# In-projection of a hybrid DiT backbone: own buffers for the mLSTM decays, and outputs that follow the states without a stop

## The chip, the cores and the metric

The kernel runs on one core of one Trainium2 chip. The metric is the device time of one execution in microseconds (us). A core has five engines that run at the same time and in their own order, and that wait for one another through semaphores: TensorE (PE, with its weight loads as PEld), VectorE (DVE), ScalarE (ACT), GpSimd (POOL) and SyncE (SP), which here issues the DMAs.

## The reference

Two layers over 1024 latent and 256 context tokens of width 1024. Each layer normalises and modulates the tokens, projects them once (`h @ w_in`) and splits the columns into attention (aq, ak, av), a bidirectional mLSTM in chunks of 128 tokens (mq, mk, mv, mo, gates) and a pooling mixer (pp); the three outputs are concatenated, projected back, and a SwiGLU follows. The part around the change is the mLSTM's chunk loop:

```
def step(carry, inp):                       # one chunk, one direction
    C, n, m = carry
    ...
    s = einsum('bhtd,bhsd->bhts', qc, kc) * exp(dmat - m_t[..., None])
    num = w_inter[..., None] * einsum('bhvk,bhtk->bhtv', C, qc) + einsum('bhts,bhsv->bhtv', s, vc)
    den = w_inter * einsum('bhk,bhtk->bht', n, qc) + sum(s, -1)
    h = num / maximum(abs(den), exp(-m_t))[..., None]
    ...
    C_new = a[..., None, None] * C + einsum('bhs,bhsv,bhsk->bhvk', wk, vc, kc)
    n_new = a[..., None] * n + einsum('bhs,bhsk->bhk', wk, kc)
def mlstm_readout(h, o_pre, ml_norm):
    hn = rms_norm(h, ml_norm)
    return hn * sigmoid(o_pre)
```

## The kernel before, in words

All matmuls are three products of f16 halves. The in-projection is a row of gemms, one after the other, which feed PE: `gemm_fm` (features by tokens, matmuls `pfm` at L492, in passes of 12 or 24) and `gemm_tm` (tokens by features, matmuls `ptm` at L497). Their order is O_MK, O_MQ, gates, O_MV, O_MO, O_MQ+P, then pooling's first half (`pool_gemm(0)`), O_AK, O_AQ 0, `pool_gemm(1)`, O_AQ 1 to 3 and last O_AV. Beside them run threads, Python generators that `spawn` puts in a list and that are stepped between pieces of a gemm; `drain(t)` steps a thread to its end at once. The kernel's own statement order and a scheduler behind it then fix the order on each engine.

The threads of the mLSTM are these. `ml_states` (`stg`) makes 18 state steps in each layer, 9 chunks by 2 directions. A step's `front` transposes k on PE (`pk`, 4 matmuls, L931), weighs it on DVE (`kw`) and splits it into f16 halves on ACT and POOL (`kh`); its `back` multiplies on PE (`pu`, 12 matmuls, L945), updates the state `C` on DVE and stores it as `snap`. `ml_outputs(z)`, z = 0 and 1, makes the outputs of the even and of the odd chunks, so the two threads go in pairs of chunks: five pairs in layer 0 (context too) and four in layer 1. One chunk (`ml_chunk`) loads its gates `sgc` and row `mrow`, multiplies q by k (`pst`), and for each direction makes the mask and bias on PE (`pm`, L998 and L999) and the exponentials `E` on ACT (L1000 and the `act` under it), weighs `pst` by E on DVE, and splits E into f16 halves `Ah` on ACT and POOL. `inter` multiplies by the state (`pxi`, L1024), `intra` multiplies `Ah` by v (`pi`, L1038), adds on DVE into `num`, makes the divisor `dn`, and the quotient `T<-num,dn`. Behind the second direction come the sum of both, the square on ACT, its sum (`s<-T`), the root on ACT and six small operations, the two gains, the split into `oh` (ACT, then DVE), and two stores `mld<-oh` (L1083), four for a pair of chunks.

Work tiles come from one pool `w` for the phase "g" (in-projection), and are freed at the start of phase "s" (attention), whose tiles lie over them. Among them is a ring `f2k` of 8 buffers of 2 KB for a partition, which holds E, `kw`, the `q` and `sqq` of the attention's keys and queries (`c_qk`), and others; a new tile waits until the readers of the tile 8 before are done. PSUM has 8 banks in this phase.

In phase "s" the mLSTM's and pooling's outputs are read back (`DMA_TRANSPOSE T<-mld` at L1317, `T<-pld`, `X<-xs`), and the attention goes by units: scores on PE (`Sp`, L1337), their maximum on DVE (`mx<-Sp`), the exponentials on ACT (`pf`), f16 halves (`phl`), a transpose by DMA (`pT<-phl`, L1366), the product with v (`pv`, L1379). The out-projection (`pwo`, L1400) fills PE between units. It needs `T<-mld` and `T<-pld`. DMAs on SP's queue are issued in the order that is written. In the views a tile's name stands without its number, and one name can cover several tiles: `T<-mld` is the part of `mixT`, and `T`, `X` are also other work tiles.

Of the kernel before, what the change touches and what calls it, by code (L numbers as in the profile page):

```python
# [9 lines left out]
F32 = mybir.dt.float32  # L10
# [8 lines left out]
P = 128  # L19
# [62 lines left out]
def hybrid_kernel(ctx: ExitStack, tc: tile.TileContext, I, out, dbg=None):  # L82
    nc = tc.nc
    order = mybir.DependencyInfo(mybir.DependencyClass.NoSync, mybir.DependencyReason.DATA)
    row = {"on": False, "last": None}

    class InRow:

        def __init__(self, e):
            self.e = e  # L90

        def __getattr__(self, name):
            f = getattr(self.e, name)

            def call(*a, **k):
                b = f(*a, **k)  # L96
                if row["on"]:
                    if row["last"] is not None:
                        tc.add_manual_dep(b.ins, row["last"].name, order, reason="written order")
                    row["last"] = b.ins  # L100
                return b
            return call

    def in_row(on):
        row.update(on=on, last=None)

    V = InRow(nc.vector)
    S, G, TE, DMA = nc.scalar, nc.gpsimd, nc.tensor, nc.sync
    MUL, ADD, SUB, MAX, MIN = ALU.mult, ALU.add, ALU.subtract, ALU.max, ALU.min
    dbg = dbg or {}  # L110

# [4 lines left out]


    cur = {}
    F2K = {"g": 8, "s": 6}
    PFB, PHB, PTB = 2, 3, 5  # L120

    def phase(kind):
# [19 lines left out]
    def bank(name="bk"):  # L142
        return cur["b"].tile([P, 512], F32, tag="bk", name=name)
# [8 lines left out]
    def pt_(shape, dt, tag, bufs=1, name=None):  # L152
        return cur["w"].tile(list(shape), dt, tag=tag, name=name or tag, bufs=bufs)

    def f2k(shape=(P, 512), dt=F32, name="f2k"):
        return pt_(shape, dt, "f2k", F2K[cur["kind"]], name)

# [33 lines left out]
    def stt(o, a, s, b, o0, o1):  # L191
        V.scalar_tensor_tensor(o, a, s, b, op0=o0, op1=o1)

    def tt(o, a, b, op, e=None):
        (e or V).tensor_tensor(o, a, b, op=op)  # L195

# [5 lines left out]
    threads = []  # L202

    def spawn(gen):
        threads.append(gen)
        return gen
# [12 lines left out]
    def pump(n=1):  # L219
        for _ in range(n):  # L220
            for g in list(threads):
                try:
                    next(g)
                except StopIteration:
                    threads.remove(g)

    def drain(g=None):
        while (g in threads) if g is not None else threads:
            if g is None:
                pump()  # L230
            else:
                try:
                    next(g)
                except StopIteration:
                    threads.remove(g)
# [16 lines left out]
    def x_tile(i):  # L252
# [3 lines left out]
        for g in range(2):  # L256
# [6 lines left out]
            else:  # L263
                V.tensor_copy(o, i_)

# [18 lines left out]
    cs_f = con.tile([P, 16], F32, name="cs_f")  # L284
    V.tensor_scalar(cs_f, cvec, -85.0, None, op0=MAX)
    act(cs_f, cs_f, AF.Exp, scale=-1.0)
    V.tensor_scalar(cs_f, cs_f, 1.0, None, op0=ADD)
    V.reciprocal(cs_f, cs_f)
    tt(cs_f, cs_f, cvec, MUL)
# [248 lines left out]
    def rstd(ms, n, u, r0=None):  # L538

        if r0 is None:  # L540
            r0 = f2k((P, 512), F32, "r0")
        act(r0[:, :n], ms, AF.Ln, bias=epsc)
        act(r0[:, :n], r0[:, :n], AF.Exp, scale=-0.5)
        act(u[:, :n], r0[:, :n], AF.Square)
        stt(u[:, :n], ms, EPS, u[:, :n], ADD, MUL)
        V.tensor_scalar(u[:, :n], u[:, :n], -0.5, 1.5, op0=MUL, op1=ADD)
        tt(r0[:, :n], r0[:, :n], u[:, :n], MUL)
        return r0
# [218 lines left out]
    for l in range(DEPTH):  # L767
        last = l == DEPTH - 1
# [203 lines left out]
        def ml_outputs(z):  # L972
            for c in range(z, nto, 2):
                yield from ml_chunk(c, z)

        def ml_chunk(c, z):
# [19 lines left out]
            def decay_(d):  # L996
                pm = bank("pm")
                mm(pm.rearrange("p (h t) -> p h t", h=4), idb, mskb[:, d].unsqueeze(1).to_broadcast([P, 4, P]), start=True, stop=False)  # L998
                mm(pm, one3, mrow[d], start=False, stop=True)  # L999
                E = f2k((P, 4, P), F32, "E")  # L1000
                for i, h in enumerate(HO):
                    r = d * 64 + c * 4 + h
                    act(E[:, i], pm[:, i * P:(i + 1) * P], AF.Exp, bias=tmq[:, 0, r:r + 1])
                Ev = E.rearrange("p h t -> p (h t)")
                for g in range(2):
                    stt(Ev[:, g * 256:(g + 1) * 256], pst[g][:, 0:256], 1.0 / 16, Ev[:, g * 256:(g + 1) * 256], MUL, MUL)
                Ah = pt_((P, 2, 4, P), F16, "Ah", 4)
                act(Ah[:, 0].rearrange("p h t -> p (h t)"), Ev)
                tt(Ah[:, 1], E, Ah[:, 0], SUB, G)
                Ahs.append(Ah)  # L1010
# [137 lines left out]
        def q_roots():  # L1148

            v = rq[:, :, :nto].rearrange("p a c h -> p a (c h)")  # L1150
            rstd(v[:, 0], nto * 8, v[:, 2], v[:, 1])
            V.tensor_scalar(v[:, 0], v[:, 1], 0.125 / 16, None, op0=MUL)
            V.tensor_scalar(v[:, 1], v[:, 1], -0.125 / 16, None, op0=MUL)
# [28 lines left out]
        def pool_tile(i, u):  # L1182
            S2, S4, S8, S16 = (1, 0), (1, 1), (2, 2), (4, 4)
            for (t0, n) in blks:
                ub = u[:, pcol(t0) - 8:pcol(t0) + n + 8]
                bA = pt_((P, 768), F32, "pb", 2, "bA")
                bB = pt_((P, 768), F32, "pb", 2, "bB")

                def win(o, s, sh, lo_, hi_, x):

                    tt(o[lo_:hi_, x:n + 16 - x], s[lo_:hi_, x - sh[0]:n + 16 - x - sh[0]],
                       s[lo_:hi_, x + sh[1]:n + 16 - x + sh[1]], ADD, G)

                if i == 0:
                    win(bA, ub, S2, 64, 128, 7)
                    win(bB, ub, S2, 0, 64, 8)
                    win(bB, bA, S4, 64, 128, 8)
                    fin = [bB, bB]
                else:
                    win(bA, ub, S2, 0, 128, 1)  # L1200
                    win(bB, bA, S4, 0, 128, 2)
                    yield
                    win(bA, bB, S8, 0, 128, 4)
                    win(bB, bA, S16, 64, 128, 8)
                    fin = [bA, bB]
                p = f2k((P, 512), F32, "pm")
                for g in range(2):
                    ps = slice(64 * g, 64 * g + 64)
                    f = fin[g][ps, 8:8 + n]
                    if t0 != 512:  # L1210
                        tt(f[:, 0:8], f[:, 0:8], edge[ps, i, 0:8], MUL, G)
                    if t0 != 0:
                        tt(f[:, n - 8:n], f[:, n - 8:n], edge[ps, i, 8:16], MUL, G)
                yield
                for g in ([0] if fin[0] is fin[1] else range(2)):
                    ps = slice(0, P) if fin[0] is fin[1] else slice(64 * g, 64 * g + 64)
                    stt(p[ps, :n], fin[g][ps, 8:8 + n], invw[ps, i:i + 1], ub[ps, 8:8 + n], MUL, SUB)
                yield
                pb = bank("ppool")
                mm(pb[:, :n], pw[:, i], p[:, :n], start=True, stop=True)  # L1220
                sc = ps16[:, l * 2 + i:l * 2 + i + 1]
                ph = f2k((P, 2, 512), F16, "ph")
                act(ph[:, 0, :n], pb[:, :n], scale=sc)
                stt(ph[:, 1, :n], pb[:, :n], sc, ph[:, 0, :n], MUL, SUB)
                DMA.dma_start(out=pld[:, i, :, t0:t0 + n], in_=ph[:, :, :n])
                yield
# [6 lines left out]
        for (t0, n) in BLOCKS:  # L1233
            if t0 in nx:
                drain(nx.pop(t0))
            for r in range(3):
                if t0 >= T and last and r == 2:
                    continue
                if l == 0 and t0 < T:
                    pb = pf0[r][t0 // 512]  # L1240
                else:
                    pb = bank("pfm")
                    fm(pb[:, :n], wf[r], h1, t0, n)
                held.append((r, t0, n, pb))
                pb = None
# [3 lines left out]
            while held and t0 > 0:  # L1249
                r_, t_, n_, pb = held.pop(0)  # L1250
                fst[r_](t_, n_, pb[:, :n_])
                pb = None
                pump()
        w = w_get(("in", l, O_MG))
        pb = bank("pmg")
# [11 lines left out]
        stg = ml_states()  # L1267
# [17 lines left out]
        for i in range(2):  # L1285
            DMA.dma_start(out=cst[i], in_=I["t_cs"][:, i])
        gemm_fm(O_MQ + P, blks, c_ml(qml, 1, INV * 4))
        drain(stg)
        spawn(ml_outputs(0))
        spawn(ml_outputs(1))  # L1290
        def pool_gemm(i):
            u = pool_u()

# [15 lines left out]
        while next_is_ada() or pend:  # L1309
            ada_fill()  # L1310
        drain()
        q_roots()


# [151 lines left out]
        for i in range(nu + 5):  # L1466
# [5 lines left out]
            if turns:  # L1472
                qt, g = turns.pop()
# [290 lines left out]
        sg, Sg, Su = sgs[0], f0.pop("Sg"), f0.pop("Su")  # L1764
        f0.clear()
        act(sg[:, :NTq], Sg[:, :NTq], AF.Silu, scale=INV)
        in_row(True)
        stt(sg[:, :NTq], Su[:, :NTq], 1.0 / SW, sg[:, :NTq], MUL, MUL)

        ho = h_ops()  # L1770
# [20 lines left out]
        for _ in ho:  # L1791
            pass
        drain()
        in_row(False)
        for k in range(4):
            split2(h2[:, k, :, H1], scv[:, k], V)

# [204 lines left out]
        for bi, (t0, n) in enumerate([(0, 512), (512, 256), (768, 256)] if last else blks):  # L2002
            sums = None if last else Sums(t0, n)
            for m in range(NK):
                w = piece("last", m)
                pb = bank("pdn")
# [8 lines left out]
            if bi == 0:  # L2015
# [3 lines left out]
                pb = None  # L2019
# [48 lines left out]
```

## Time and profile before

| | |
|---|---|
| median of 3 runs | 2776.61 us (2774.57 to 2776.82) |
| the profiled execution | 2780.47 us |
| its span | 2778.7 us |
| PE busy | 2564.7 us, 92% of the span |
| DVE busy | 1890.2 us, 68% |
| ACT busy | 1387.1 us, 50% |
| POOL busy | 1269.3 us, 46% |
| TensorE clock granted, mean | 0.969 |

The span is what the profiler sees of the program, and the rest of the execution, 1.8 us, lies around it. The profiled execution is 3.9 us above the median of the three runs. PE is the busiest engine; the clock that it was granted is given as a share of full speed.

### The profile page before, as it was taken

How to read it: one execution, taken by the hardware profiler on the slowest of the kernel's cores; microseconds unless marked ns; L12 is line 12 of the kernel's file. 1: busy time of each engine (PE TensorE's matmuls, PEld its weight loads, DVE VectorE, ACT ScalarE, POOL GpSimd, SP SyncE). 2: the span in 40 equal slices, each digit the busy share in tenths (PEclk: the TensorE clock that was granted, in tenths of full speed). 3: DMA queues.
4: the chain of work that ended last, by engine and by line, in shares of the span. 5: the costliest groups of instructions: out<-in, count | busy, mean ns of one | idle time of the engine just before them, and what ended most of it. 6: DMA issues, size and time to landing. Idle time of an engine off the chain costs nothing. (4 is left out here: it accounts for less than half of the span.)

```text
span 2778.7 us, 53623 instructions
## 1 busy us (share of the span) xinstructions
PE 2564.7 (92%) x21403; PEld 1500.9 (54%) x21403; DVE 1890.2 (68%) x3233; ACT 1387.1 (50%) x2650; POOL 1269.3 (46%) x963
## 2 busy tenths in 40 slices
PE   7999989987899999999999998888878899999997
PEld 4875556655555555555554684455545344444444
DVE  5558867778766555656565557866777767667676
ACT  5345557766443434444344544466765444444453
POOL 1124446774334435444443213456763465555651
PEclk9999999999899999999999999999989899999999
DMA  9544489995132222223212222389993111111211
GB/s 301 144 123 113 126 203 184 190 177 121 57 92 81 87 84 84 86 82 92 61 46 78 69 55 57 115 185 182 191 174 102 46 53 54 62 61 54 61 53 76
DMA packets 631629, 296.21 MB, mean 107 GB/s; under 512 B 362888, under 2 KB 620756, under 8 KB 630868
## 3 DMA queue, kind: packets, MB, share of 16 engines
q1 hardware_dynamic: 631204, 292.73, 42.9%
q8 instruction: 167, 2.74, 0.4%
q14 instruction: 82, 0.67, 0.1%
q10 hardware_dynamic: 176, 0.07, 0.0%
HBM read 176.19 MB, written 20.87 MB: 71 GB/s over the span
## 5 line engine op out<-in xcount | busy, mean ns | idle before, releaser
L1960 PEld LDWEIGHTS <-hlp 128*128 128x128 f16 x5040 | 492.0, 98 | 602.7 <-issue 26.6
L1960 PE MATMUL Swb<-T,hlp 128*128 128x512 f16 x1920 | 445.6, 381 | 18.5 <-DVE sg L96 13.0
L195 POOL TENSOR_TENSOR phl<-pf,phl 128x1280 f16<-128x1280 f32 (+1 forms) x132 | 345.2, 2618 | 176.8 <-ACT phl L175 123.1
L96 DVE SCALAR_TENSOR_TENSOR hlp<-ws,hlp 128x512 f16<-128x512 f32 (+1 forms) x320 | 231.6, 732 | 112.0 <-ACT hlp L175 89.2
L175 ACT ACTIVATE hlp<-ws 128x512 f16<-128x512 f32 (+1 forms) x320 | 162.6, 518 | 210.7 <-PE Swb L1960 90.5
L175 ACT ACTIVATE pf<-Sp,mx,rq 128x1280 f32<-128x1280 f32 (+1 forms) x144 | 189.6, 1317 | 118.1 <-DVE mx L96 98.8
L96 DVE TENSOR_REDUCE mx<-Sp 128x1 f32<-128x1280 f32 (+1 forms) x132 | 195.0, 1477 | 63.4 <-PE Sp L1337 55.4
L1960 PE MATMUL Swb<-tq,hlp 128*128 128x512 f16 x960 | 223.4, 382 | 8.0 <-DVE hlp L96 4.6
L1960 PE MATMUL Swc<-T,hlp 128*128 128x512 f16 x960 | 227.2, 379 | 0.0
L1400 PE MATMUL pwo<-T,hl 128*128 128x512 f16 (+1 forms) x960 | 194.5, 354 | 34.0 <-DVE X L96 14.3
L492 PE MATMUL pfm<-T,hl 128*128 128x512 f16 (+1 forms) x1032 | 216.4, 363 | 4.2 <-ACT E L175 4.1
L1337 PE MATMUL Sp<-T 128*128 128x512 f16 (+1 forms) x800 | 169.3, 348 | 42.5 <-ACT pf L175 40.1
L96 DVE SCALAR_TENSOR_TENSOR hlp<-st,hlp 128x256 f16<-128x256 f32 (+1 forms) x201 | 149.0, 746 | 86.7 <-ACT hlp L175 73.8
L195 POOL TENSOR_TENSOR ws<-st 128x256 f32<-128x256 f32 (+1 forms) x97 | 104.4, 1083 | 170.1 <-DMA st<-in_w_ffn_down_dram 67.9
L175 ACT ACTIVATE T<-sg 128x512 f16<-128x512 f32 (+1 forms) x170 | 98.8, 599 | 165.0 <-POOL sg L195 96.3
L1972 PE MATMUL dx<-T,hlp 128*128 128x256 f16 x1440 | 177.3, 273 | 1.0 <-DVE hlp L96 1.0
L195 POOL TENSOR_TENSOR X<-X,T 128x512 f32<-128x512 f32 x80 | 114.1, 1427 | 139.8 <-DVE X L96 105.1
L1960 PE MATMUL Swa<-T,hlp 128*128 128x512 f16 x720 | 169.3, 380 | 0.0
L1972 PEld LDWEIGHTS <-hlp 128*128 128x128 f16 x1440 | 139.1, 100 | 33.1 <-issue 4.8
L1400 PEld LDWEIGHTS <-hl 128*128 128x128 f16 x960 | 97.7, 102 | 109.8 <-issue 40.8
L175 ACT ACTIVATE phl<-pf 128x1280 f16<-128x1280 f32 (+1 forms) x115 | 144.6, 1262 | 21.2 <-DMA pT<-phl 18.9
L195 POOL TENSOR_TENSOR sg<-sg,T 128x512 f32<-128x512 f32 x60 | 88.7, 1478 | 143.6 <-DVE T L96 143.2
(308 smaller groups left out, 4735.8 us busy)
## 6 DMA issues: line engine op xcount, KB each, us to landing
T<-in_w_ada_dram SPq DMA_DIRECT2D x48, 512.0 KB
rawa<-in_w_ada_dram SPq DMA_DIRECT2D x48, 512.0 KB
st<-in_w_in_dram SPq DMA_DIRECT2D x32, 512.0 KB
st<-in_w_out_dram SPq DMA_DIRECT2D x64, 256.0 KB
st<-in_w_ffn_gate_dram SPq DMA_DIRECT2D x32, 512.0 KB
st<-in_w_ffn_up_dram SPq DMA_DIRECT2D x30, 512.0 KB
st<-in_w_ffn_down_dram SPq DMA_DIRECT2D x30, 512.0 KB
xs<-X SPq DMA_DIRECT2D x4, 2048.0 KB
```

The costliest lines, as they stand in the source:

```text
L96: b = f(*a, **k)
L175: b = S.activation(o, i, f, **kw).ins
L195: (e or V).tensor_tensor(o, a, b, op=op)
L492: mm(o, w[:, a, k, :], h[:, k, b, t0:t0 + n], start=(k == 0 and j == 0), stop=(k == nk - 1 and j == 2))
L1337: mm(Sp[:, e * nk + b0:e * nk + b0 + m], ql, qkv[:, 4 + h // 4, a, k0 + b0:k0 + b0 + m], start=(a == 0), stop=(a == 1), skip_group_check=True)
L1400: mm(pb, w[:, a, k, :], mixT[:, k0 + k, b, t0:t0 + n], start=(k == 0 and j == 0), stop=(k == 3 and j == 2))
L1960: mm(o, w[:, a, k, :], B[:, b], start=(s in "172" and k == 0 and j == 0), stop=(k == kh(i) - 1 and j == 2), skip_group_check=True)
L1972: mm(dbank[i][:, r * 256:(r + 1) * 256], w[:, a, k, :], B[:, b], start=(first and k == 0 and j == 0), stop=(not first and k == kh(i) - 1 a ...
```

## The change

Three things are changed. First, `E` gets a tag of its own with 2 buffers, in place of a tile in the ring, and the ring has 7 buffers in place of 8 in phase "g" (pooling's work tiles are shortened to make room). Second, after the gemm of O_MQ+P the state thread is not stepped to its end any more. A thread `outputs` waits for it and then starts the two output threads, while the next gemms go on. Third, a wrapper that can keep an engine's instructions in written order now serves two engines under names; the list of names for the in-projection, `INROW`, is empty, and the SwiGLU names VectorE as before.

```diff
-    F2K = {"g": 8, "s": 6}
+    F2K = {"g": 7, "s": 6}
+    INROW = ()
...
-                E = f2k((P, 4, P), F32, "E")
+                E = pt_((P, 4, P), F32, "E", 2)
...
-                bA = pt_((P, 768), F32, "pb", 2, "bA")
-                bB = pt_((P, 768), F32, "pb", 2, "bB")
+                bA = pt_((P, 528), F32, "pb", 2, "bA")
+                bB = pt_((P, 528), F32, "pb", 2, "bB")
...
         gemm_fm(O_MQ + P, blks, c_ml(qml, 1, INV * 4))
-        drain(stg)
-        spawn(ml_outputs(0))
-        spawn(ml_outputs(1))
+        in_row(True, *INROW)
+
+        def outputs():
+            while stg in threads:
+                yield
+            spawn(ml_outputs(0))
+            spawn(ml_outputs(1))
+
+        spawn(outputs())
...
         drain()
+        in_row(False, *INROW)
         q_roots()
```

How the order on the engines changes is shown at three places. A line number of the changed program is 2 higher than before up to the in-projection's end, and 9 higher in the attention.

First, PE in layer 1, at the end of a state step behind the gemm of O_MQ+P (`kh` and X are the step's tiles, `hl` a gemm's weights). Before:

```order
L945 LDWEIGHTS kh
L945 MATMUL pu<-X,kh 64x65
L931 LDWEIGHTS X
L931 MATMUL pk<-id_127,X 128x128
L931 LDWEIGHTS X
L931 MATMUL pk<-id_127,X 128x128
```

And after:

```order
L947 LDWEIGHTS kh
L947 MATMUL pu<-X,kh 64x65
L494 LDWEIGHTS hl
L494 MATMUL pfm<-T_72,hl 128x512
L494 LDWEIGHTS hl
L494 MATMUL pfm<-T_72,hl 128x512
```

Where one state step stood directly behind another, 12 matmuls of the next gemm stand between them now, behind nearly every one of the last nine steps of layer 1 and in the same way at the last steps of layer 0. The instructions and their number stay the same. The first output pair's `pst` comes later for it: in layer 0 behind the first pooling gemm and one and a half tiles of O_AK, in layer 1 behind all of O_AK and half of the first O_AQ.

Second, PE in layer 1, the last matmuls ahead of the attention's first scores. Before:

```order
L497 MATMUL ptm<-hl,T_72 128x128
L497 LDWEIGHTS T_72
L497 MATMUL ptm<-hl,T_72 128x128
L1337 LDWEIGHTS T_73
L1337 MATMUL Sp<-T_73 128x512
```

And after:

```order
L1040 MATMUL pi<-X,Ah 128x65
L1040 LDWEIGHTS Ah
L1040 MATMUL pi<-X,Ah 128x65
L1346 LDWEIGHTS T_73
L1346 MATMUL Sp<-T_73 128x512
```

The last pair's `pi` (24 matmuls, and its `pxi` and first `pi` before them) stood ahead of the whole O_AV gemm (`ptm`, 48 and 192 matmuls) and stands behind it now. In layer 0 the 24 `pi` of the last pair stood ahead of the O_AV gemm too, and now have only its last 48 `ptm` behind them.

Third, DVE and SP in layer 1 at the same place. DVE before:

```order
L96 TENSOR_TENSOR oh<-T_73,oh 128x256
L96 COPY rq<-msq 128x4x2
L96 STREAM_SHUFFLE sqq<-q 128x512
L96 TENSOR_TENSOR sqq<-sqq,cst 128x512
...
L96 SCALAR_TENSOR_TENSOR T_73<-ptm,T_73 128x256
L96 SCALAR_TENSOR_TENSOR hl<-st,hl 128x512
L96 TENSOR_REDUCE mx<-Sp 128x1
```

And after:

```order
L96 TENSOR_TENSOR T_73<-T_73,s_22084 128x256
L96 TENSOR_SCALAR s_22107<-s_22107 128x4
L96 TENSOR_TENSOR T_73<-T_73,sgc 128x256
L96 TENSOR_TENSOR s_22107<-s_22107 128x4
L96 TENSOR_TENSOR T_73<-T_73,s_22107 128x256
L96 TENSOR_TENSOR oh<-T_73,oh 128x256
L96 TENSOR_TENSOR T_73<-T_73,sgc 128x256
L96 TENSOR_TENSOR oh<-T_73,oh 128x256
L96 TENSOR_REDUCE mx<-Sp 128x1
```

SP before:

```order
L1083 DMA mld<-oh 128x256 x4
L396 DMA st<-in_w_out_dram 128x4x128
L1165 DMA T_73<-sqq 64x512 x8
L1317 DMA_TRANSPOSE T_72<-mld 128x2x1024 x2
L1319 DMA T_72<-pld 128x2x1024 x2
```

And after:

```order
L1167 DMA T_73<-sqq 64x512 x4
L1330 DMA X<-xs 128x2x1024
L1328 DMA T_72<-pld 128x2x1024 x2
L1330 DMA X<-xs 128x2x1024 x3
L1085 DMA mld<-oh 128x256 x4
L398 DMA st<-in_w_out_dram 128x4x128
L1326 DMA_TRANSPOSE T_72<-mld 128x2x1024 x2
```

On DVE the last pair's whole closing chain moved to the place directly ahead of the first maximum `mx<-Sp`, in both layers. On SP the four last stores `mld<-oh` stood 8 DMAs and more ahead of the transposes that read them, and now have one weight load between. In the changed program the first `mx`, `pf` and `phl` of each layer's attention wait also for the landing of these four stores, for DVE's last `oh` and POOL's last `Ah`, since their tiles lie over the pool in which `oh` and `Ah` are read last; before, that pool's last readers were others. POOL has no instruction of its own between the last `Ah` and the first `phl`, in either layer.

## Rows read from the trace of the kernel before

**Rows 1.** The page's first part: busy time by engine, with shares and instruction counts.

```profile
PE 2564.7 (92%) x21403; PEld 1500.9 (54%) x21403; DVE 1890.2 (68%) x3233; ACT 1387.1 (50%) x2650; POOL 1269.3 (46%) x963
```

**Rows 2.** Windows over layer 0's output pairs: us, busy times, PEclk, DMA share, GB/s.

```profile
230.00:269.00 39.00, 35.72 (x332) 21.14 (x328) 34.09 (x94) 22.46 (x57) 16.70 (x20) 0.91 0.42 113
...
298.00:336.00 38.00, 34.74 (x342) 21.90 (x338) 30.04 (x86) 18.53 (x47) 18.74 (x21) 0.96 0.37 105
...
sum 184.40, PE 175.23 PEld 109.26 DVE 147.77 ACT 94.62 POOL 72.13; mean PE 29.21 PEld 18.21 DVE 24.63 ACT 15.77 POOL 12.02
```

**Rows 3.** Windows over layer 1: the states, four output pairs, the O_AV gemm.

```profile
1655.00:1674.00 19.00, 16.48 (x171) 8.32 (x169) 12.63 (x36) 7.11 (x20) 5.51 (x8) 0.82 0.11 29
...
1703.40:1739.20 35.80, 30.90 (x236) 15.52 (x235) 28.55 (x77) 19.48 (x47) 13.61 (x12) 0.95 0.23 61
1739.20:1773.80 34.60, 30.15 (x231) 14.79 (x230) 30.00 (x78) 15.50 (x39) 17.95 (x18) 0.90 0.27 70
1773.80:1797.00 23.20, 20.36 (x182) 11.15 (x181) 18.49 (x46) 12.12 (x30) 8.44 (x6) 0.85 0.49 154
...
sum 166.10, PE 147.89 PEld 82.37 DVE 132.19 ACT 79.38 POOL 62.49; mean PE 24.65 PEld 13.73 DVE 22.03 ACT 13.23 POOL 10.41
```

**Rows 4.** Waits of PE, 1655 to 1830: us in total, times, longest.

```profile
PE pfm L492 <- ACT E L175: 4.1, 1, 4.1
PE pxi L1024 <- ACT E L175: 4.1, 3, 2.0
...
PE pu L945 <- POOL kh L195: 1.5, 5, 0.5
```

**Rows 5.** Waits of ACT, 1650 to 1830.

```profile
ACT E L175 <- POOL q L195: 5.3, 1, 5.3
```

**Rows 6.** PE's timeline in layer 1: two passes of 12 matmuls of a gemm.

```profile
1676.20 2.76 PE L492 MATMUL pfm<-T,hl 128*128 128x512 f16 x12
...
1711.65 4.44 PE L492 MATMUL pfm<-T,hl 128*128 128x512 f16 x12 [4.09 <-ACT E L175]
```

**Rows 7.** Timeline of PE, DVE and SP at the start of layer 0's attention.

```profile
361.62 10.88 PE L497 MATMUL ptm<-hl,T 128*128 128x128 f16 x192
...
374.71 1.49 DVE L96 TENSOR_REDUCE mx<-Sp 128x1 f32<-128x1280 f32 x1 [0.55 <-PE Sp L1337]
...
372.14 8.59 SPq L1317 DMA_TRANSPOSE T<-mld  x2
...
382.25 5.76 SPq L1366 DMA_TRANSPOSE pT<-phl  x1
```

**Rows 8.** The same at the start of layer 1's attention (PE, SP).

```profile
1809.30 10.88 PE L497 MATMUL ptm<-hl,T 128*128 128x128 f16 x192
...
1818.82 4.30 SPq L1317 DMA_TRANSPOSE T<-mld  x2
...
1829.46 3.09 SPq L1366 DMA_TRANSPOSE pT<-phl  x1
```

**Rows 9.** DVE by groups, 189 to 380: busy us, mean ns of one, idle before.

```profile
L96 DVE TENSOR_TENSOR T<-num,dn 128x256 f32<-128x256 f32 x20 | 15.1, 765 | 0.1
...
L96 DVE TENSOR_TENSOR s<-s 128x4 f32<-128x4 f32 x30 | 6.5, 227 | 0.3 <-ACT s L175 0.2
...
L96 DVE TENSOR_TENSOR T<-T,s 128x256 f32<-128x256 f32 x10 | 4.2, 416 | 0.0
```

**Rows 10.** DVE and ACT timeline near the end of layer 0's last pair.

```profile
354.27 1.49 DVE L96 TENSOR_TENSOR T<-num,dn 128x256 f32<-128x256 f32 x1
...
364.77 0.40 ACT L175 ACTIVATE oh<-T 128x256 f16<-128x256 f32 x1
```

**Rows 11.** POOL's timeline beside it.

```profile
353.71 1.77 POOL L195 TENSOR_TENSOR q<-q,cst 128x512 f32<-128x512 f32 x1 [5.75 <-DVE dn L96]
```

**Rows 12.** Start of the program: a DMA of SP's queue and its first reader.

```profile
1.54 0.36 SPq L273 DMA_DIRECT2D idn<-in_t_idn_dram  x1
...
3.34 0.17 DVE L96 COPY sel<-idn 128x2 f32<-128x2 f32 x1 [3.34 <-DMA idn<-in_t_idn_dram]
```

More of the change, by code (lines that the diff above doesn't have):

```diff
@@ L84, in hybrid_kernel, with __init__ @@
     order = mybir.DependencyInfo(mybir.DependencyClass.NoSync, mybir.DependencyReason.DATA)
-    row = {"on": False, "last": None}
+    rows = {}
     class InRow:
-        def __init__(self, e):
-            self.e = e
+        def __init__(self, e, name):
+            self.e, self.row = e, rows.setdefault(name, {"on": False, "last": None})
         def __getattr__(self, name):
-            f = getattr(self.e, name)
+            f, row = getattr(self.e, name), self.row
             def call(*a, **k):
@@ L102, in __getattr__, with in_row @@
             return call
[L104 to L108, printed above, removed]
+    def in_row(on, *names):
+        for name in names:
+            rows[name].update(on=on, last=None)
+    V, S = InRow(nc.vector, "V"), InRow(nc.scalar, "S")
+    G, TE, DMA = nc.gpsimd, nc.tensor, nc.sync
     MUL, ADD, SUB, MAX, MIN = ALU.mult, ALU.add, ALU.subtract, ALU.max, ALU.min
@@ L1766, in hybrid_kernel @@
         act(sg[:, :NTq], Sg[:, :NTq], AF.Silu, scale=INV)
-        in_row(True)
+        in_row(True, "V")
         stt(sg[:, :NTq], Su[:, :NTq], 1.0 / SW, sg[:, :NTq], MUL, MUL)
@@ L1793, in hybrid_kernel @@
         drain()
-        in_row(False)
+        in_row(False, "V")
         for k in range(4):
```

## The prediction

> **What bounds the kernel now.** I read the page first: PE is busy 92% of the span and no other engine above 68% [rows 1], so time can only be won where PE stands still or runs at less than full clock, and only lost by making it stand longer. The change moves work in the two in-projections and at the attention's two starts, so the second view is the windows over these stretches; the reader sees in them PE's idle time (length less busy time) and PEclk. In layer 0 PE is idle for 184.40 − 175.23 = 9.2 us [rows 2]. The clock was granted at 0.91 for 39 us and at 0.96 for 38 us, a loss of 0.09 × 39 + 0.04 × 38 = 5 us beside full clock. In layer 1 the idle time is 166.10 − 147.89 = 18.2 us, and the clock costs 0.18 × 19.0 + 0.05 × 35.8 + 0.10 × 34.6 + 0.15 × 23.2 = 12 us [rows 3]. So some 14 us are to be had in layer 0 and 30 us in layer 1. The third view, the waits of PE, says for what it stands in layer 1: E, 4.1 us at one gemm pass and 4.1 us at three `pxi` [rows 4]. ACT's waits trace the first back: E had waited 5.3 us for POOL's `q` to give back a buffer of the ring [rows 5]. The last view is the timeline at the attention's start, where PE waits for one chain and every us of it counts.
>
> **The change: gains.** (1) The states are no longer run in one block. In layer 1 that block is the stretch 1655 to 1674: PE is idle 19.00 − 16.48 = 2.5 us, of which waits for `kh` (1.5 in five) are the most [rows 3, 4], and the clock loses 3.4. With 12 matmuls (2.76 at full clock [rows 6]) between two steps, the longest of those waits, 0.5, is covered. I take 5 of these 5.9 us. In layer 0 the block is shorter and none of the low clocks lies in it [rows 2]; I take 0. The price is from 0 (another thread is late instead) to 5.9.
>
> (2) E's own buffers. The one wait that is surely the ring's cost PE 4.09 us, and the pass behind it ran 4.44 against 2.76, together 4.09 + 1.68 = 5.8 us [rows 6]. With its own two buffers, E waits only for POOL's `Ah` of two E's before. The three `pxi` waits (4.1) show no ring wait behind them: there ACT came late with its own queue, so I count none of them. The ring itself loses one buffer and four E's of each pair, so the others have more room; I take 0 for that.
>
> (3) The outputs start later and lie beside other gemms. The work per pair is the same, so what matters is how dense it is beside the passes of PE. In layer 1 the four pairs now begin behind all of O_AK: one long stretch with PE work and little else, then three stretches as dense as before (DVE 18.5 to 30.0 us in 23 to 36 [rows 3]), so I leave their stalls as they are but for one: the stretch from 1739, where DVE is 30.00 of 34.6 us busy and PE idle 4.4, is spread out. I take 1 us of it, and 2 of layer 0's 14, whose five pairs stay about as dense. Bounds: 0, and the whole idle time and clock loss, 44 less what (1) and (2) take.
>
> Gains: 5 + 5.8 + 1 + 2 = 14 us.
>
> **The change: losses.** The last pair's end now stands on the path into the attention. Before, it was hidden by O_AV's 48 + 192 matmuls (10.88 us for the 192 [rows 7, 8]). Now that cover is gone in layer 1 (no matmul behind the last `pi`), and in layer 0 48 are left, by the same rate 10.88/4 = 2.7 us. What must run behind the last `pi`: on DVE, seven operations of 128x256 for each of two chunks (into `num`, quotient, sum, sum of squares, two gains, `oh`). At 0.416 each [rows 9] that is 14 × 0.416 = 5.8. The small ones, three for `dn` and six for the root, two chunks, are 18; at the 227 ns of their largest group [rows 9] they would be 4.1, and as they overlap one another I take 2.3. Three hops over ACT (square, root, `oh`), at 0.40 each [rows 10] and a little between, are 1.4. Sum 9.5 us. Then the four stores: the first three are issued beside the chain, and the last lands after 3.34 − 1.54 = 1.8 us, if it is like the first DMA of the program [rows 12]; I find no closer row, so 1 to 2.7 (two issues of 0.36 more) bound it. The first `mx` is now behind that landing: 9.5 + 1.8 = 11.3 us after the last `pi`.
>
> Layer 0: O_AV ended at 361.62 + 10.88 = 372.5, `mx` began at 374.71, 2.2 later, and the first `pT` at 382.25, 9.75 later [rows 7]. Now `mx` comes 11.3 − 2.7 = 8.6 after O_AV's end. The transposes `T<-mld` can't be issued ahead of the same stores, and hold SP's queue for 8.59 [rows 7], with the `pT` behind them in the queue: 8.6 + 8.6 = 17.2, against 9.75. Loss 7.4. Layer 1: `pT` came 1829.46 − 1820.18 = 9.3 after O_AV's end; taking its `mx` at 2.2 as in layer 0, 7.1 after `mx`. `T<-mld` takes 4.30 [rows 8] and is done before that. Now: 11.3 + 7.1 = 18.4. Loss 9.1. Behind the waiting `mx` on DVE, `pf` on ACT and `phl` on POOL stands the whole attention, and behind the transposes on SP all `pT`. PE has no other work there: the out-projection needs `T<-mld`, and scores go only two units ahead. What it gets back is small (the loads of `T<-pld` no longer follow the transposes); I leave it out. Losses 7.4 + 9.1 = 16.5, say 16; from 12 (the chain overlaps better, landing 1) to 22.
>
> One rule speaks for a longer chain. Beside a POOL operation of 1.77 us [rows 11] the quotient took 1.49 us [rows 10], and its mean is 765 ns against 416 of a like operation [rows 9]. If all ten operations of the chain with two inputs in SBUF went at 765, the losses would be 10 × 0.35 × 2 = 7 us more. I take 416, since POOL has nothing between the last `Ah` and `phl`. The Trainium skill, SBUF — State Buffer, section "SBUF: two separate sides", says that VectorE and GpSimd share a port pair as an exclusive lock, and that an operation with two SBUF inputs can be blocked for a whole GpSimd instruction; by that the row of 1.49 us is explained, and a chain without POOL beside it would run at the shorter time.
>
> **Sum.** 2780.47 − 14 + 16 = 2782.5 for an execution like the profiled one, which lay 3.9 us above the median of the runs shown: 2778.6 beside that median. I say 2778.5, a change of +2 us.
>
> **The rivals.** *Faster: the stalls mostly go.* With E out of the ring, the `q`, `sqq` and `kw` of the keys and queries wait less too, and a pair that comes with a gemm behind it never stops PE, as in layer 1's first pass at 2.76 [rows 6]; with the idle time goes the clock's loss. Then 20 of layer 1's 30 us and 6 of layer 0's 14 are won, and the losses are nearer 14: −12, 2764.5. For it speaks that idle time and lost clock stand together in the same windows [rows 3]; against it, that only one slot wait is in ACT's waits. The Trainium skill, Perfetto Trace Analysis, section "Optimization Strategy", says that the same gap repeated on an engine that should be full can mean too few buffers; by that, the three `pxi` gaps would go too, 4.1 us more.
>
> *Slower: two buffers are too few for E.* A third E must wait for `Ah` on POOL, which goes in order. When a `q` stands ahead of that `Ah` and waits for its own input, E waits for POOL just as it did for the ring, at the same 4.09 + 1.68. If the one wait stays and one pair more gets it, the sum is +2 + 11.6, 2790. It decides from one such wait on; against it speaks that an E's four exponentials, weighing and `Ah` take some 4 us (1.77 for POOL's part by the row of a like operation [rows 11]) and that a pass of 2.76 us [rows 6] lies between a pair's second and third E.
>
> *Nothing.* The outputs' start is hidden, the chain is not: both sums are small, 2776.
>
> **How the numbers follow.** What a measurement can tell from no change is 0.2%, 5.5 us. Forecast 0.42 (2774 to 2784 as its own range), faster rival 0.32, slower rival 0.20, nothing 0.06. Faster by over 0.2%: 0.32 and 0.03 of the forecast, 0.35. Slower: 0.20 and 0.06, 0.26. Within: 0.39. The range leaves out one tenth at each end: the faster rival can reach below 2764 if the pairs of layer 1 lose all stalls, the slower above 2790 if the chain goes at 765 ns as well.
>
> **What would show it.** Right: in the window of layer 1 after O_MQ+P no idle PE between `pu` and `pfm` and PEclk 1.00; no wait of E for `q`; the first `mx` of each attention named as waiting for a DMA of `oh`, 8 to 11 us after O_AV's last matmul, and `pT` at 17 to 18. Wrong: `mx` as early as before (the losses are off), E waiting for POOL's `Ah` (the slower rival), or PE idle in layer 1's pairs below 6 us (the faster one). The step that I trust least is (3).

## The result, and the profile after

The changed kernel takes 2793.59 us (median of 6 runs, 2790.06 to 2797.38) against 2776.72 for the kernel before (6 runs): the ratio is 1.006, 95% interval 1.0047 to 1.0073, so it is 16.9 us slower. The prediction said 2778.5 and at most 2790. Its profiled execution took 2793.64 us, with a span of 2791.6 (before: 2778.7). Between the two traces the difference is thus 12.9 us, less than between the medians, since the traced execution of before lay 3.75 us above its median.

The page's first part of the changed kernel, the answer to [rows 1]:

```profile
PE 2574.9 (92%) x21403; PEld 1512.7 (54%) x21403; DVE 1884.5 (68%) x3233; ACT 1386.2 (50%) x2650; POOL 1269.6 (45%) x963
```

The instructions of these engines are the same in number, and yet PE is busy 10.2 us longer: matmuls took longer, and the mean granted clock is 0.964 instead of 0.969. To see where, I set the same marks in both traces: the decays' matmul `pdec` (where the states begin), the first `pst` (the first output pair), the first `Sp` (the attention), and the last `pv` (the attention's end). Windows of the kernel before, layer 0 and layer 1, each from `pdec` to `pst` and from there to `Sp` (length; busy times of PE, PEld, DVE, ACT, POOL; PEclk; DMA share; GB/s):

```profile
122.84:198.79 75.95, 75.52 (x1229) 61.25 (x1227) 39.57 (x100) 28.27 (x71) 12.76 (x18) 1.00 0.48 135
198.79:373.43 174.64, 165.87 (x1729) 104.17 (x1725) 141.12 (x399) 90.82 (x237) 69.43 (x73) 0.97 0.44 125
...
1610.79:1674.03 63.24, 60.72 (x893) 46.74 (x891) 34.93 (x85) 24.95 (x56) 12.98 (x18) 0.95 0.22 59
1674.03:1821.11 147.08, 131.38 (x1167) 74.05 (x1167) 119.56 (x317) 72.29 (x176) 56.98 (x53) 0.94 0.32 94
```

The same four of the changed kernel:

```profile
124.41:218.03 93.62, 93.62 (x1369) 71.62 (x1367) 46.84 (x106) 32.94 (x81) 21.76 (x29) 1.00 0.45 127
218.03:390.37 172.34, 157.75 (x1586) 99.78 (x1585) 126.65 (x378) 84.18 (x221) 59.81 (x62) 0.91 0.40 113
...
1627.47:1712.74 85.27, 84.39 (x1022) 59.02 (x1021) 48.91 (x99) 34.60 (x73) 25.97 (x32) 1.00 0.22 60
1712.74:1831.11 118.37, 103.92 (x1038) 61.32 (x1037) 99.98 (x279) 60.40 (x152) 46.30 (x39) 0.93 0.31 91
```

The states between the gemms do what they should: the stretch ahead of the first pair has no idle PE in layer 0, 0.9 us in layer 1, and full clock. But in layer 0 the stretch ends 17.7 us later (93.6 against 75.9), and the outputs' own stretch gives back only 2.3 of it (172.3 against 174.6): 15.4 us are lost up to the first scores. In idle time and clock: before, 0.4 + 8.8 us idle and 0.03 × 174.6 = 5.2 of clock; after, 14.6 idle and 0.09 × 172.3 = 15.5. Two thirds of the loss is clock in this trace. In layer 1 the first stretch grows by 22.0 and the second shrinks by 28.7: 6.7 us are won.

The waits of PE in layer 0's output stretch, 180 to 400 us of the changed kernel (us in total, times, longest):

```profile
PE pxi L1026 <- ACT sqq L96: 2.8, 1, 2.8
PE pm L1000 <- DVE E L96: 2.1, 1, 2.1
PE pxi L1026 <- DVE T L96: 2.0, 1, 2.0
PE ppool L1222 <- DVE pm L96: 1.9, 1, 1.9
PE Sp L1346 <- DVE T L96: 1.7, 1, 1.7
```

They are spread over all pairs, and no single one explains the loss. The last pair is new: its `pxi` (2.0) and the scores (1.7) wait in the stretch that holds only O_AV.

Then the attention's start. The timeline of PE, DVE and SP of the changed kernel, layer 0:

```profile
385.81 2.84 PE L499 MATMUL ptm<-hl,T 128*128 128x128 f16 x48
...
396.86 1.49 DVE L96 TENSOR_REDUCE mx<-Sp 128x1 f32<-128x1280 f32 x1 [2.56 <-DMA mld<-oh]
...
393.53 1.77 SPq L1085 DMA_DIRECT2D mld<-oh  x4
...
396.30 8.37 SPq L1326 DMA_TRANSPOSE T<-mld  x2
404.76 6.29 SPq L1375 DMA_TRANSPOSE pT<-phl  x2
```

And layer 1:

```profile
1827.32 0.90 PE L1040 MATMUL pi<-X,Ah 128*128 128x65 f16 x24
...
1839.96 1.49 DVE L96 TENSOR_REDUCE mx<-Sp 128x1 f32<-128x1280 f32 x1 [2.05 <-DMA mld<-oh]
...
1836.18 2.15 SPq L1085 DMA_DIRECT2D mld<-oh  x4
...
1839.59 4.03 SPq L1326 DMA_TRANSPOSE T<-mld  x2
1847.02 3.08 SPq L1375 DMA_TRANSPOSE pT<-phl  x1
```

In layer 0 O_AV ends at 388.65, `mx` begins 8.2 us later and `pT` 16.1 later; in layer 1 `mx` begins 11.7 and `pT` 18.8 us after the last `pi`. `mx` waits for the landing of the stores by name. Before, these were 2.2 and 9.75 in layer 0 and 9.3 for `pT` in layer 1 [rows 7, 8]. So the chain is on the path, at the size that was worked out. At the attention's end, counted from the first `Sp`, 295.0 − 291.8 = 3.2 us of it are left in layer 0 and 278.9 − 274.9 = 4.0 in layer 1.

### The profile page after: what moved, and what is told of

It reads as the page before. It is cut to its first block, busy times and chain, and to the rows that moved or that the text cites. A ratio compares the mean times of both kernels' runs of the same rounds, so it can differ in the third digit from the quotient of the medians.

```text
span 2791.6 us, 53653 instructions
## 1 busy us (share of the span) xinstructions
PE 2574.9 (92%) x21403; PEld 1512.7 (54%) x21403; DVE 1884.5 (68%) x3233; ACT 1386.2 (50%) x2650; POOL 1269.6 (45%) x963
## 5 line engine op out<-in xcount | busy, mean ns | idle before, releaser
L197 POOL TENSOR_TENSOR sg<-sg,T 128x512 f32<-128x512 f32 x60 | 89.4, 1490 | 147.2 <-DVE T L96 146.9
L1388 PEld LDWEIGHTS <-pT 128*128 128x128 f16 x3936 | 136.6, 99 | 32.0 <-issue 8.0
```

The source lines that it names most:

```text
L1388: mm(self.qs[0][:, h * 64:h * 64 + 64], self.pT[:, a, e * nkt + kt], qkv[:, 6, b, self.k0 + kt * P:self.k0 + (kt + 1) * P][:, kv * 64:kv * ...
```

## Experiments

The loss in layer 0's projections was not forecast. Theory L says that the late start of the outputs costs it. The rival, theory B, says that the buffers do: two for E, and a ring with seven. The first four experiments part the two, and the layers.

**Only the buffers**, with the block of states (against the changed kernel):

```diff
-        def outputs():
-            while stg in threads:
-                yield
...
-        spawn(outputs())
+        drain(stg)
+        spawn(ml_outputs(0))
+        spawn(ml_outputs(1))
```

> Only the buffers are changed: E has its own two, the ring has 7, the states are run in one block as before. Theory L (the late start of the outputs cost the 15 us of layer 0): 2770 to 2776, the first scores of layer 0 near 373 us, and layer 1 without the 5.3 us wait of E. Theory B (two buffers for E and a ring of 7 cost it, by new waits for POOL): 2785 to 2792, with the first scores of layer 0 near 385 or later.

Measured: 2784.48 us, ratio 1.0029 (1.0017 to 1.0041). Between the ranges, just below theory B's, and the first scores of layer 0 come at 379.3 us, between the two as well: the buffers alone cost some 8 us, about half. ACT's waits show how. First the kernel before, in layer 0's output stretch and in layer 1 (1640 to 1822), then this kernel in the same two places:

```profile
ACT sqq L175 <- POOL q L195: 3.6, 3, 2.1
...
ACT sqq L175 <- POOL q L195: 4.1, 2, 3.1
```

```profile
ACT sqq L96 <- POOL q L197: 6.8, 3, 3.4
...
ACT sqq L96 <- POOL q L197: 9.5, 2, 5.0
```

E no longer waits for POOL's `q` (5.3 us in layer 1 before [rows 5]), but `sqq`, which stayed in the ring, waits in its place, and longer. This reaches PE: in layer 1 its wait of 4.1 us for E at a gemm pass [rows 4] is 0.3 here, and its matmul `msq`, which reads `sqq`, waits instead. PE's wait at `msq` in layer 1 before, in this kernel, and in the one with a ring of 8 that follows below:

```profile
PE msq L1091 <- ACT sqq L175: 1.9, 1, 1.9
...
PE msq L1093 <- ACT sqq L96: 6.1, 2, 4.2
...
PE msq L1093 <- ACT sqq L96: 1.9, 1, 1.9
```

**Only the later outputs**, E in a ring of 8:

```diff
-    F2K = {"g": 7, "s": 6}
+    F2K = {"g": 8, "s": 6}
...
-                E = pt_((P, 4, P), F32, "E", 2)
+                E = f2k((P, 4, P), F32, "E")
```

> Only the start of the outputs is changed: they follow the states without a stop, and E stays in the ring of 8. Theory L: 2788 to 2797, the first scores of layer 0 near 388 to 392 us. Theory B: 2772 to 2780, first scores near 376.

Measured: 2792.98 us, ratio 1.0059 (1.0041 to 1.0076). The whole loss is there without the buffers, as theory L says; layer 0's first scores come at 386.9 us, 1 us ahead of its range.

**The thread in layer 1 alone**, and **in layer 0 alone** (the other layer with the block; buffers as changed):

```diff
-        spawn(outputs())
+        if l == 1:
+            spawn(outputs())
+        else:
+            drain(stg)
+            spawn(ml_outputs(0))
+            spawn(ml_outputs(1))
```

> The buffers as in the change, the outputs follow without a stop in layer 1 alone, layer 0 runs its states in one block. Theory L: layer 0 as before, layer 1 wins some 7 us up to its first scores and loses 4 in its attention: 2770 to 2776. Theory B: layer 0 is as slow as in the changed kernel: 2788 to 2794.

> The buffers as in the change, the outputs follow without a stop in layer 0 alone, layer 1 runs its states in one block. Theory L: the whole loss of layer 0 stays (15 us in the projections, 3 in the attention) and layer 1 has at most the gain of its own E buffers: 2788 to 2796. Theory B: the same within the error as the first experiment of this call.

Measured: 2778.19 us, ratio 1.0018 (1.0007 to 1.0029), for layer 1; 2794.23, ratio 1.0074 (1.0056 to 1.0092), for layer 0. Beside the buffers alone, at 1.0029, the thread costs 0.45% in layer 0, some 12 us, and wins 0.1%, some 3 us, in layer 1 (not clear of the error). The expectation for layer 0 held; for layer 1 it was 2 us low, by what the buffers cost.

**A ring of 8 beside E's own buffers** (block of states):

```diff
-    F2K = {"g": 7, "s": 6}
+    F2K = {"g": 8, "s": 6}
...
-        sa = wk.tile([P, P], F32, tag="sa", name="sa", bufs=2) if n == P else f2k((P, 2 * P), F32, "sa")
+        sa = wk.tile([P, P], F32, tag="sa", name="sa", bufs=1) if n == P else f2k((P, 2 * P), F32, "sa")
```

> As the first experiment (E has its own two buffers, the states run in one block), but the ring keeps its 8 buffers; the room comes from the small tile sa, one buffer in place of two. If the ring's eighth buffer is what the own buffers cost in layer 0: its projections come back to 174 to 176 us from the first pst to the first scores (180 with a ring of 7), ACT's waits for POOL's q fall, and the time is 2768 to 2776. If two buffers for E are too few: 179 to 181 and 2780 to 2787 as there.

Measured: 2779.06 us, ratio 1.0 (0.9991 to 1.0009). The time lies between the two expected ranges, beside a kernel before that took 2778.70. The eighth buffer of the ring takes back what the own buffers cost, and no more: E's buffers are worth nothing that can be measured. What the missing second buffer of `sa` costs was not run by itself, so a small gain could be hidden behind it. In layer 1 the wait at `msq` is back to 1.9 us, and from `pdec` to `Sp` it takes 207.3 us (208.9 with a ring of seven, 210.3 before). In layer 0 the expected drop to 176 us was not seen in this profiled execution (178.1 from `pst` to `Sp`, 179.6 with seven), and `sqq` still waits 5.7 us for POOL's `q` there, so the place of most of those 8 us is not shown by the traces.

**The late start by itself**, on the kernel before: its block of states, E in the ring, and the outputs as many steps late as in the changed kernel.

```diff
         drain(stg)
-        spawn(ml_outputs(0))
-        spawn(ml_outputs(1))
+
+        def outputs():
+            for _ in range(5 if l == 0 else 7):
+                yield
+            spawn(ml_outputs(0))
+            spawn(ml_outputs(1))
+
+        spawn(outputs())
```

> The kernel before, with its block of states and E in the ring, but the outputs begin as many steps later as in the changed kernel. If the late start alone costs it: 2792 to 2800 (the block's 6 us of layer 1 are paid as well), the first scores of layer 0 at 386 to 391. If it is the states that lie between the gemms: 2774 to 2780.

Measured: 2796.05 us, ratio 1.0066 (1.0051 to 1.008). The late start is enough for a loss of this size. But the block is paid here too, so the times don't tell what the states between the gemms win or cost. And the loss lies elsewhere in this kernel's traced execution, which is 3.4 us below its median: layer 0's first scores come at 381.9 us, not at 386 to 391, so that layer 0 loses 6.9 us up to them where the changed kernel loses 15.4, and layer 1 wins 1.1 where that wins 6.7. Layer 0's output stretch here, and with only the later outputs (the second experiment), where the states lie between the gemms and pooling's work tiles are shorter:

```profile
219.38:381.91 162.53, 148.90 (x1585) 95.10 (x1585) 130.72 (x378) 83.74 (x221) 58.85 (x62) 0.97 0.42 120
...
216.76:386.92 170.16, 155.05 (x1586) 98.42 (x1585) 130.42 (x378) 83.83 (x221) 59.76 (x62) 0.92 0.40 114
```

The idle time is nearly the same (13.6 and 15.1 us), the clock is not. That the states between the gemms cost nothing in layer 0 is therefore not shown.

**States early, outputs in time.** If the start is the fault, the block can be removed without it: a second thread steps the states, so that they are done by the end of O_MQ+P.

```diff
+        def boost(n):
+            for _ in range(n):
+                if stg in threads:
+                    try:
+                        next(stg)
+                    except StopIteration:
+                        threads.remove(stg)
+                yield
...
+        spawn(boost(5 if l == 0 else 8))
         gemm_tm(O_MO + P, nto, c_mo(1))
```

> The kernel before, but a second thread steps the states twice a piece from the second O_MO gemm on, so that they are done without a block and the outputs begin where they began before. If the block is worth its 5.9 us in layer 1 and nothing stands against it: 2768 to 2772. If the steps then crowd the gemms of O_MO and the gain goes: 2775 to 2779.

Measured: 2770.45 us, ratio 0.9968 (0.9956 to 0.998): 0.32% faster than the kernel before, as expected. Its windows in layer 1, from `pdec` to `pst` and on to `Sp`:

```profile
1607.54:1664.24 56.70, 56.70 (x893) 45.46 (x891) 34.42 (x85) 24.32 (x56) 13.08 (x18) 1.00 0.24 64
1664.24:1812.50 148.26, 133.79 (x1168) 74.94 (x1168) 120.10 (x317) 72.09 (x176) 57.15 (x53) 0.93 0.33 95
```

The first is 63.24 − 56.70 = 6.5 us shorter than before, with no idle PE and full clock, so the block was worth what was worked out and a little more (5.9 at most); layer 0's is 1.3 shorter (74.6 against 75.9).

**With E's own buffers and a ring of 8 too:**

```diff
-        sa = wk.tile([P, P], F32, tag="sa", name="sa", bufs=2) if n == P else f2k((P, 2 * P), F32, "sa")
+        sa = wk.tile([P, P], F32, tag="sa", name="sa", bufs=1) if n == P else f2k((P, 2 * P), F32, "sa")
...
-                E = f2k((P, 4, P), F32, "E")
+                E = pt_((P, 4, P), F32, "E", 2)
```

(the ring keeps its 8 buffers, and pooling's work tiles have 528 columns, as in the change)

> The one before with E's own two buffers and a ring of 8 (one buffer of sa). If both gains add: 2760 to 2768. If the own buffers are worth nothing even with 8 in the ring: as the one before.

Measured: 2771.16 us, ratio 0.9971 (0.996 to 0.9983). The gains don't add; E's buffers are worth nothing here too. Its traced execution took 2779.97 us, 8.8 above this kernel's median, and its layer 0 needed 185.3 us from `pst` to `Sp` at a clock of 0.94, where the kernel with the early states alone needed 174.6 at 0.97. One trace may thus be some 10 us off in such a stretch, and the sizes by layer in this document stand on one execution of each kernel.

Why does a late start cost? Theory C: the last pair's chain loses the gemm that covered it. Theory D: the pairs take the same time wherever they lie, so each us of delay costs one. **Half the delay** tells them apart, since 192 matmuls of O_AV are still behind the last `pi` then:

```diff
-            for _ in range(5 if l == 0 else 7):
+            for _ in range(2 if l == 0 else 3):
```

> The kernel before with its block of states, the outputs begin late by half as many steps as in the late start: three and four in place of six and eight, so that the last pair still has 192 matmuls of the O_AV gemm behind its last pi. Theory C (what costs is that the last pair has no gemm left to cover it): 2774 to 2781, and the attention's first mx where it was before. Theory D (each us of a later start costs, since the pairs take the same time wherever they lie): half of 18, 2784 to 2789.

Measured: 2780.98 us beside 2780.49, ratio 1.0008 (0.9999 to 1.0018). Theory D's 2784 to 2789 is out by the ratio (1.0018 is 5 us at most). The trace says more. Its output stretches of layer 0 and layer 1:

```profile
209.39:379.60 170.21, 158.29 (x1645) 98.37 (x1642) 136.81 (x397) 87.95 (x232) 64.77 (x70) 0.95 0.42 118
1690.80:1820.63 129.83, 118.19 (x1120) 68.19 (x1120) 113.08 (x316) 69.59 (x173) 53.08 (x50) 0.96 0.34 98
```

From `pdec` to `Sp` layer 0 takes 255.5 us, 4.9 more than before, and layer 1 takes 201.9, 8.4 less. So within the cover a later start is won in layer 1 and part of it is lost in layer 0 already: theory C holds for the sum and for layer 1, and is not the whole of layer 0. The expectation that `mx` would begin where it did was wrong as well: it also waits for the stores here, 3.85 us after the first `Sp` in layer 0 (1.3 before):

```profile
383.45 1.49 DVE L96 TENSOR_REDUCE mx<-Sp 128x1 f32<-128x1280 f32 x1 [3.14 <-DMA mld<-oh]
```

**The wait for the stores.** In the changed kernel `oh` is put where the attention's pool does not lie over it:

```diff
-            oh = pt_((P, 2, 256), F16, "kho", 4, "oh")
+            oh = spare[:, (2 * z + 1) * 256:(2 * z + 2) * 256].bitcast(F16).rearrange("p (a e) -> p a e", a=2)
```

> The changed kernel, but oh lies in a tile that is not under the attention's pool, so the first mx, pf and phl no longer wait for the landing of the last four stores; the transposes of mld still do. If that wait is what the attention's start costs: each attention wins 3 to 5 us, 2783 to 2788. If the transposes behind the stores set the end anyway: 2790 to 2795.

Measured: 2792.08 us, ratio 1.005 (1.0037 to 1.0062), not told apart from the changed kernel's 1.006. Layer 0's timeline of PE, DVE and SP in this kernel:

```profile
390.74 2.32 PE L1346 MATMUL Sp<-T 128*128 128x512 f16 x12 [1.74 <-DVE T L96]
...
393.94 1.49 DVE L96 TENSOR_REDUCE mx<-Sp 128x1 f32<-128x1280 f32 x1 [0.19 <-DVE T L96]
...
398.16 7.21 SPq L1326 DMA_TRANSPOSE T<-mld  x2
405.47 10.11 SPq L1375 DMA_TRANSPOSE pT<-phl  x3
```

`mx` comes 3.2 us after `Sp` where it came 6.5 after, and no longer waits for a DMA. But `pT` comes 14.7 us after `Sp` as it came 14.4 after: it stands behind `T<-mld` on SP's queue, which waits for the stores with or without the pool. The free `mx` also went ahead of the last `oh` on DVE, so that `T<-mld` is issued 7.4 us after `Sp` in place of 5.9. The wait for the landing was priced rightly, and it has a second one behind it.

**The changed kernel with a ring of 8** (one buffer of `sa`, as above):

> The changed kernel with a ring of 8 (one buffer of the small tile sa in place of two). If the ring's eighth buffer is worth its 5 to 8 us here too: 2784 to 2789. If the late start hides it, since other waits take its place: 2790 to 2796.

Measured: 2793.05 us, ratio 1.0052 (1.0039 to 1.0065). With the late start the eighth buffer is worth nothing that can be told: the two costs don't add.

**Early states, and in layer 1 a start four steps late**, within the cover:

```diff
         drain(stg)
+
+        def outputs():
+            for _ in range(3):
+                yield
+            spawn(ml_outputs(0))
+            spawn(ml_outputs(1))
+
+        if l == 0:
+            spawn(ml_outputs(0))
+            spawn(ml_outputs(1))
+        else:
+            spawn(outputs())
-        spawn(ml_outputs(0))
-        spawn(ml_outputs(1))
```

(on the kernel with the early states)

> The early states in both layers, and in layer 1 alone the outputs begin four steps late, so that 192 matmuls of O_AV still cover the last pair. Theory C (only the lost cover costs; in layer 1 a start within the cover gives denser pairs, as the half-late start's 201.9 us from the decays to the first scores against 210.3 of before showed): 2763 to 2768, layer 1 at 196 to 200 us. Theory D (a later start costs by itself): 2773 to 2778.

Measured: 2769.73 us beside 2778.2, ratio 0.996 (0.9944 to 0.9975). Layer 1, from `pdec` to `pst` and on to `Sp`:

```profile
1610.32:1677.37 67.05, 67.05 (x940) 50.16 (x939) 35.72 (x86) 26.46 (x59) 17.20 (x22) 1.00 0.22 59
1677.37:1808.41 131.04, 118.03 (x1120) 68.32 (x1119) 111.20 (x316) 69.59 (x173) 52.59 (x50) 0.96 0.34 97
```

The sum, 198.1 us, is as expected, 6.9 less than with the early states alone (205.0). The time is just above the expected range, beside a kernel before that took 1.5 us more than at first. In the time the two kernels can't be told apart (0.996 and 0.9968), so this last gain stands in one trace only. Both are faster than the kernel before and than the changed one.

The traces of the main kernels between the same marks, in us (differences of the start times of the marks; the attention from its first `Sp` to the end of its last `pv`):

| kernel | L0 pdec to pst | L0 pst to Sp | attention | to L1's pdec | L1 pdec to pst | L1 pst to Sp | attention |
|---|---|---|---|---|---|---|---|
| before | 75.9 | 174.6 | 291.8 | 945.6 | 63.2 | 147.1 | 274.9 |
| changed | 93.6 | 172.3 | 295.0 | 942.1 | 85.3 | 118.4 | 278.9 |
| buffers only | 76.0 | 179.6 | 290.6 | 943.9 | 60.6 | 148.3 | 273.3 |
| later outputs only | 93.6 | 170.2 | 295.6 | 942.5 | 85.3 | 120.8 | 279.0 |
| thread in layer 0 alone | 93.6 | 171.7 | 294.4 | 942.1 | 61.6 | 148.0 | 273.0 |
| late start only | 95.0 | 162.5 | 296.2 | 942.6 | 88.6 | 120.6 | 278.3 |
| half late | 85.3 | 170.2 | 293.1 | 946.0 | 72.1 | 129.8 | 273.2 |
| early states | 74.6 | 174.6 | 292.9 | 942.8 | 56.7 | 148.3 | 273.7 |
| early states, E's buffers | 74.6 | 185.3 | 290.3 | 944.2 | 56.7 | 146.9 | 272.4 |
| early, layer 1 late | 74.6 | 174.7 | 292.2 | 946.0 | 67.1 | 131.0 | 273.5 |

## Why the prediction was wrong

The forecast was +2 us, from 14 of gains and 16 of losses; it is +16.9.

- *The step that failed* is (3), that the pairs "stay about as dense" in layer 0 and win 2 us there. Layer 0's projections lost 15.4 us up to the first scores, more than the 12.9 between the two traces, and 12.1 to 15.5 in each of the five traced kernels whose outputs follow the states without a stop in layer 0. The prediction counted the late start only as a lost cover at the attention, and took it that work moved ahead of the first pair would come off the pairs' stretch. In layer 1 it did (22.0 later, 28.7 shorter), in layer 0 it did not (17.7 later, 2.3 shorter). The late start alone reproduces the loss in time (1.0066), and the thread in layer 0 alone does too (0.45% on top of the buffers); in its own trace the late start alone has 6.9 us of it in layer 0's projections.
- *Step (1)*, the block of states, was right: 5 of 5.9 us were claimed, and the early states show 6.5 in layer 1 and 1.3 in layer 0, 0.32% in all. In layer 1 the changed kernel shows it as well: up to the first pair 0.9 us idle at full clock, where before it was 2.5 at 0.95.
- *Step (2)*, E's own buffers, was wrong: 5.8 us of gain were claimed, and they bring nothing that can be measured with a ring of 8 (1.0) and cost 8 us with a ring of 7 (1.0029). The wait that was priced, 4.1 us of PE behind E, did go, and with a ring of 7 it came back at `msq` behind `sqq` (4.2). That "the others have more room" was taken at 0 and was the opposite.
- *The losses* were right as a mechanism and in their first size: `mx` at 8.2 and 11.7 us (8.6 and 11.3 forecast), `pT` at 16.1 and 18.8 (17.2 and 18.4). The landing of the stores, put at 1.8, took 2.6 and 2.1 us; its upper bound is 2.5 by its own terms, not 2.7. What the losses cost at the attention's end was mis-sized: 3.2 and 4.0 us from the first scores against 16. The rest was given back within the attention; that it would not be was assumed. It is luck that the forecast was not further off: a loss put some 9 us too high made up for part of the gains that did not come.
- *The rivals.* The slower one had the right sign and nearly the time (2790), by luck, for a cause that the runs exclude: the later outputs without E's buffers are as slow, and E's two buffers with a ring of 8 cost nothing where the outputs start in time. The wait that it names is in the changed kernel, though (ACT's E waits 2.9 us once in layer 0 for POOL's `Ah`). The faster one leaned on the rule that repeated gaps can mean too few buffers (the Trainium skill, Perfetto Trace Analysis, "Optimization Strategy"). Here that was at most a part of it: with buffers of its own, E still made three `pxi` wait in layer 1 of the changed kernel, 2.4 us in place of 4.1.

Open: why layer 0's pairs did not get shorter. Theory D, a cost for each us, is excluded by the half delay; theory C explains the attention's start and the last pair's own waits (2.0 and 1.7 us), some 7 and 4 us. The rest is mostly the clock in layer 0's output stretch: it is 0.90 to 0.93 in all five kernels whose outputs follow the states there without a stop, and 0.97 in the late start alone, with nearly the same idle time (14.6 us in the changed kernel, 13.6 there). What those five share beside the late start is the states between the gemms and pooling's shorter work tiles; the tiles alone don't lower it (0.96 with only the buffers changed), so the states may have a part in it. Which stall lowers the clock in one and not in the other was not found, and each is one trace.

## What to carry to other kernels

Removing a stop by starting the work behind it later can cost more than the stop: ask first what covers the end of that work, and whether the stage that it enters gets shorter by as much as it starts later. Better to finish the work ahead of the stop sooner, so that nothing behind it moves (here 0.32% faster, where the change was 0.6% slower). A buffer taken from a shared ring can be paid by the ring's other users (8 us here with the block of states, nothing that can be told with the late start); look at all that wait for it, not at the tile that waits longest.

## What was not expected of the hardware

Most of the time lost in layer 0 between the two traces was clock and not idle time: idle time rose by 5.4 us (9.2 to 14.6), and the loss at the granted clock by 10.3 (5.2 to 15.5), with PE's mean granted clock over the whole program at 0.963 to 0.965 in all six runs of the changed kernel and at 0.966 to 0.972 in the runs of the kernel before that were made beside the experiments.
